# A two-pass projection for the eight decay and gate columns of a hybrid decoder layer

## The chip, the cores and the metric

The kernel runs on one core of a Trainium2 chip. The core has a matrix engine (PE, with its weight loads shown apart as PEld), three engines for work on vectors (DVE, ACT and POOL) and sixteen DMA engines. In this kernel nearly all DMAs are issued from the queue of a fifth engine, SP. The engines run side by side and wait for one another through semaphores. The metric is the device time of one execution in microseconds (us); lower is better.

## The reference

One decoder layer with a sequence of 2048 tokens and 1024 channels. One input projection feeds two kinds of mixers, four heads each: a gated delta rule (GDN) and HGRN2. After them come the output projection, an MLP of width 4096 and a gated embedding. The columns that this case is about are `a_gdn` and `b_gdn`, four each: they become the decay and the gate of the four GDN heads.

```python
hn = rms_norm(h, pre_mix_norm[i])
proj = jnp.einsum('btd,dc->btc', hn, w_in[i]).astype(f32)
qkv = proj[..., OFF_GDN_QKV:OFF_GDN_Z]
a_gdn = proj[..., OFF_GDN_A:OFF_GDN_B]          # 4 columns
b_gdn = proj[..., OFF_GDN_B:OFF_HG_F]           # 4 columns
...
beta = jax.nn.sigmoid(b_gdn)
g_dec = -jnp.exp(gdn_a_log[i]) * jax.nn.softplus(a_gdn + gdn_dt_bias[i])
o_a = gated_delta_rule_chunked(q_a, k_a, v_a, g_dec, beta)
...
o_b = hgrn2_chunked(jax.nn.silu(q_hg), k_b, i_hg, log_f)
```

Everything is float32.

## The kernel before

**Products in parts.** A float32 operand is split into a high part `t[:, 0]`, rounded to the PE's format, and a low part `t[:, 1]`, the rest (`split`, line 164 on ACT and line 165 on DVE). A product of 128 output columns, 1024 input channels and 512 tokens takes for each of the eight blocks `k` of 128 channels three matmuls of 128x512: high weight with high input, high weight with low input, low weight with high input. That is 24 matmuls into one PSUM bank.

**Quarters and works.** The tokens are cut into four quarters of 512. The loop over `works` (lines 1053 to 1077) makes, for each quarter, 33 such products: first `ab`, the eight columns for decays and gates (padded to 128: the decays in rows 0 to 3 of the result, the gates in rows 32 to 35), and then, for each head number `h` from 0 to 3, the eight products k, q, v, z of a GDN head and f, i, q, g of an HGRN2 head. The result of a work lies in one of two PSUM banks (`pm`, two buffers), so the work after the next can start only when the bank has been read.

**Ticks.** Every work has `SPT = 3` steps of eight matmuls, and after each step `tick()` (with `half()` in the middle of it) runs what the agenda holds for this moment: a mixer is a generator, each of its pieces issues instructions, and lists of offsets (`A_STEPS` for the GDN mixer, `B_STEPS` for the HGRN2 mixer) say at which tick after the head's first work each piece stands. Thus the small matmuls of the mixers are placed by hand among the large ones. A mixer runs on for up to 64 ticks, that is 40 ticks into the 24 of the next head; the mixers of head 3 run into the next quarter, through its `ab` work and the works of its head 0.

**Order on the engines.** The order of PE's instructions, and that of SP's DMAs within the loop, is as written. On ACT, DVE and POOL a planner puts the instructions in order by its own estimate of when each can run. Once it is fixed, each engine takes its instructions in that order.

**What stands around the start of a quarter.** `decays` (lines 493 to 524) takes the `ab` result: two ACT reads of the PSUM bank (`sp`, line 498, and the gates' tanh, line 500), then a short chain that changes between DVE and ACT (`se`, lines 502 to 504, with two loads of function tables on ACT; `sp`, lines 505 and 506), a running sum on DVE (line 508), a store `gd`, a reordered copy `gbb` (line 515) and four transposes on PE (line 519). At the same ticks the last mixers of the quarter before are still in the middle. GDN head 3 does its triangular solve on DVE (`pr_g` and `xs_g`, lines 698 to 703), stores it (`xd_g`, line 708), loads it back in another layout (`xt_g`, line 715), transposes it on DVE (`xn_g`, line 717) and multiplies on PE (`psp_g`, line 722). GDN head 2 finishes (`og_g` line 585, `osq_g` line 587, `hl_g` line 165, then the matmuls `nrm_g`, lines 270 and 271). The new quarter's first convolution reads its bank with three DVE instructions (`acc_kg`, line 542).

**Weights.** In quarter 0 each work's weights are loaded raw, split, and written to DRAM as a high and a low part of 512 KB each (`cache_...<-w`); the later quarters load these 1024 KB back (`reload`). Three buffers `whl` hold weights; the weights of work `j + 2` are asked for at the start of work `j`.

Of the kernel before, what the change touches and what calls it, by code (L numbers as in the profile page):

```python
# [10 lines left out]
F32 = mybir.dt.float32  # L11
F32R = mybir.dt.float32r
BF16 = mybir.dt.bfloat16
U32 = mybir.dt.uint32
AF = mybir.ActivationFunctionType
ALU = mybir.AluOpType
# [4 lines left out]
P = 128  # L21
T = 2048
D = 1024
KD = D // P
QT = 512
# [63 lines left out]
def trunk(ctx, tc, x, xT, pT, vecs, w_in, w_ab, gdn_a_log, gdn_dt_bias, w_out, w_up, w_down,  # L89
# [345 lines left out]
    with mixers as mctx:  # L435
# [45 lines left out]
        def stage(name, src, k=KD):  # L481
# [8 lines left out]

            return ready

        def decays(ps, q):

            gb = mt(f"gb_{q}", "gb", 1, (36, QT))
            sp = m2.tile([4, QT], F32, tag="tmp", name=f"sp_{q}")
            se = m2.tile([4, QT], F32, tag="th", name=f"se_{q}")
            S.activation(sp, ps[0:4, :], AF.Identity, bias=dec[:, 1:2])
            V.memset(gb, 0.0)
            S.activation(gb[32:36, :], ps[32:36, :], AF.Tanh, scale=0.5)  # L500
            V.tensor_scalar(gb[32:36, :], gb[32:36, :], 0.5, 0.5, ALU.mult, ALU.add)
            V.scalar_tensor_tensor(se, sp, -1.0, sp, ALU.mult, ALU.max)
            S.activation(se, se, AF.Exp, scale=-1.0)
            S.activation(se, se, AF.Ln, bias=1.0)
            V.scalar_tensor_tensor(sp, sp, 0.0, se, ALU.max, ALU.add)
            V.tensor_scalar(sp, sp, nexpa, None, ALU.mult)
            for c in range(NC):
                V.tensor_tensor_scan(gb[0:4, blk(c)], one[0:4, :], sp[:, blk(c)], 0.0, ALU.mult, ALU.add)
            gd = dr.tile([4, QT], F32, name=f"gd{q}")
            decay[q] = [gd, None]  # L510
            yield
            nc.sync.dma_start(gd, gb[0:4, :])
            yield
            back = mt(f"gbb_{q}", "gbb", 1, (36, QT // 2))
            V.tensor_copy(back.rearrange("p (n b i) -> p n b i", b=NB, i=SB), odd_back(gb))
            yield
            ps = bank(f"ps_gb_{q}", ph)
            for c in range(NC):
                PE.transpose(ps[:, c * 36 : (c + 1) * 36], back[:, blk(c // 2)] if c % 2 else gb[:, blk(c)],
                             ident[:36, :36])  # L520
            gcol = sm.tile([P, NC, 36], F32, tag="gcol", name=f"gcol_{q}", bufs=2)
            V.tensor_copy(gcol.rearrange("p c n -> p (c n)"), ps[:, : NC * 36])
            V.tensor_scalar(gcol[:, :, 4:8], gcol[:, :, 0:4], -1.0, None, ALU.mult)
            decay[q][1] = gcol
# [426 lines left out]
        for q in range(NQ):  # L951
            works.append((f"ab{q}", "ab", w_ab, q, None, None, None, None))
            for h in range(4):
                g, b = {}, {}
                t = SPT * len(works)
                for j, then in KINDS:
                    works.append((f"{j}_{q}_{h}", f"in{j + h}", w_in[j + h], q, h, then, g, b))
                a_steps, b_steps = (A_LAST, B_LAST) if (q, h) == (NQ - 1, 3) else (A_STEPS, B_STEPS)
                if h:
                    a_steps = A_AHEAD + a_steps[2:]  # L960
                elif q == 0:
                    a_steps = A_FIRST + a_steps[len(A_FIRST) :]
                at(t, gdn_mixer(q, h, g), a_steps)
                at(t, turn_i(q, h, b), I_STEPS)
                at(t, hgrn_mixer(q, h, b), b_steps)
# [3 lines left out]
        def stage_work(j):  # L969

            if j < len(works) and works[j][3] == 0:
                staged[j] = stage(works[j][0], works[j][2])

        def split_work(j):

            if j < len(works):
                split_w[j] = staged.pop(j)() if j in staged else reload(works[j][1], works[j][0])

        def keep_work(j):
            if works[j][3] == 0:  # L980
                keep(works[j][1], split_w[j])

        def load_x(q):

# [53 lines left out]
                for k, n in enumerate(names):  # L1038
                    sumd[n, g] = c, k

        per_q = SPT * (1 + 8 * 4)
        starts = [per_q * q + 5 + n * i for q, m, n in ((1, 6, 14), (2, 5, 16), (3, 5, 16)) for i in range(m)]
        for g, t in enumerate(starts):
            at(t, down_sums(g), (0, 4, 6, 10))
# [7 lines left out]
        with tc.manual_schedule(engines={mybir.EngineType.SP}):  # L1052
# [5 lines left out]
            for j, (name, key, src, q, h, then, g, b) in enumerate(works):  # L1058
# [4 lines left out]
                w, xt = split_w.pop(j), xts[q]  # L1063
                terms = []
                for k, xk in enumerate(xt):
                    terms += [(w[:, 0, k, :], xk[:, 0, :]), (w[:, 0, k, :], xk[:, 1, :]), (w[:, 1, k, :], xk[:, 0, :])]
                nt = len(terms)
                for s in range(SPT):
                    for i in range(s * nt // SPT, (s + 1) * nt // SPT):
                        if i == (2 * s + 1) * nt // (2 * SPT):  # L1070
                            half()
                        PE.matmul(ps, *terms[i], start=i == 0, stop=i == nt - 1)  # L1072
                    if s == SPT - 1 and h is None:
                        at(clock[0], decays(ps, q), (0, 2, 3, 5) if q else (0, 2, 4, 7))
                    tick()
                    if s == SPT - 1 and h is not None:
                        then(ps, q, h, g, b)

            qs = (2, 3)
# [752 lines left out]
```

## Time and profile before

The three runs gave 2724.35, 2725.19 and 2733.05 us; the median is 2725.19 us. The profiled execution has a span of 2719.9 us from the first instruction to the last. No time beside its span is given for that execution; the median lies 5.3 us above the span.

| engine | busy us | share of the span | instructions |
|---|---|---|---|
| PE | 2660.8 | 98% | 12745 |
| PEld | 2215.1 | 81% | 12745 |
| DVE | 2040.8 | 75% | 4219 |
| ACT | 1464.0 | 54% | 2940 |
| POOL | 118.5 | 4% | 133 |

The works of the projection run from 40 us to 1064 us. The `ab` works begin at 40.2, 285.5, 544.05 and 805.4 us. The rest of the span is output projection, MLP and gate.

How to read it: a row of the timeline has the start in us, the duration in us, the engine, the line, the operation, what it writes and reads, its shape, and in brackets how long the engine sat idle before it and what ended that. A row of waits has who waited for whom, the total in us, how often, and the longest. A row of windows has the stretch, its length, and then for each engine the busy time in it. A PE row with "x16" is a run of sixteen matmuls.

### The profile page before, as it was taken

How to read it: one execution, taken by the hardware profiler on the slowest of the kernel's cores; microseconds unless marked ns; L12 is line 12 of the kernel's file. 1: busy time of each engine (PE TensorE's matmuls, PEld its weight loads, DVE VectorE, ACT ScalarE, POOL GpSimd, SP SyncE). 2: the span in 40 equal slices, each digit the busy share in tenths (PEclk: the TensorE clock that was granted, in tenths of full speed). 3: DMA queues.
4: the chain of work that ended last, by engine and by line, in shares of the span. 5: the costliest groups of instructions: out<-in, count | busy, mean ns of one | idle time of the engine just before them, and what ended most of it. 6: DMA issues, size and time to landing. Idle time of an engine off the chain costs nothing.

```text
span 2719.9 us, 38475 instructions
## 1 busy us (share of the span) xinstructions
PE 2660.8 (98%) x12745; PEld 2215.1 (81%) x12745; DVE 2040.8 (75%) x4219; ACT 1464.0 (54%) x2940; POOL 118.5 (4%) x133
## 2 busy tenths in 40 slices
PE   8999999999999999998999999999999999999999
PEld 6788888888888887876788888888888888888887
DVE  7778878787777777576989867768787765567776
ACT  7665555465445455575655646555555545465432
POOL 0000000000000000011000000001000000001000
PEclk9999999999999999998999999999999999999999
DMA  8777777667666665887566457667454346577663
GB/s 282 273 237 255 236 263 242 216 214 241 213 201 221 223 213 164 271 281 231 177 232 228 175 178 240 216 202 244 164 196 163 139 172 207 193 256 247 216 212 131
DMA packets 268742, 589.24 MB, mean 217 GB/s; under 512 B 55658, under 2 KB 60232, under 8 KB 249344
## 3 DMA queue, kind: packets, MB, share of 16 engines
q1 hardware_dynamic: 266240, 582.59, 63.9%
q0 software_dynamic: 2304, 4.20, 0.9%
q8 instruction: 101, 1.65, 0.3%
q14 instruction: 97, 0.79, 0.1%
HBM read 419.75 MB, written 166.92 MB: 216 GB/s over the span
## 4 chain that ended last, share of the span: by engine, by line
PE 51%; DMA 3%; DVE 3%; issue 3%; ACT 1%; POOL 1%; SPq 0%; POOLq 0%; DVEq 0%; ACTq 0%
PE d L1143 22%; PE u L1143 22%; PE mmg L1143 6%; PE mmo L1143 1%; DMA raw_out<-in_w_out_dram 1%; DMA yo<-in_xT_dram 0%; PE mme L191 0%; POOL acc_y L234 0%; DMA b<-h1d 0%; DMA w_out<-cache_out 0%; DMA db<-hid 0%; DVE t L165 0%; DMA h1d<-yo 0%; POOL yo L1229 0%; DVE pr_g L698 0%
## 5 line engine op out<-in xcount | busy, mean ns | idle before, releaser
L1072 PE MATMUL mm<-xt,w 128*128 128x512 f32 x3072 | 784.1, 400 | 1.4 <-ACT zt_zg L577 1.1
L1072 PEld LDWEIGHTS mm<-xt,w 128*128 128x128 f32 x3072 | 553.3, 189 | 102.3 <-ACT zt_zg L577 1.5
L1143 PE MATMUL d<-db,da 128*128 128x512 f32 x2688 | 611.0, 389 | 0.5 <-ACT db L217 0.2
L1143 PE MATMUL u<-t,wu 128*128 128x512 f32 x2604 | 591.1, 389 | 0.0
L1143 PEld LDWEIGHTS d<-db,da 128*128 128x128 f32 x2688 | 504.3, 188 | 106.4 <-DVE db L218 1.0
L1143 PEld LDWEIGHTS u<-t,wu 128*128 128x128 f32 x2604 | 488.7, 188 | 101.5
L218 DVE TENSOR_TENSOR db<-db 128x512 fp32r<-128x512 f32 x224 | 159.9, 714 | 72.4 <-ACT db L217 71.7
L1495 DVE TENSOR_TENSOR u<-u,u 128x512 f32<-128x512 f32 x224 | 150.2, 681 | 58.1 <-PE u L1143 56.6
L1143 PE MATMUL mmo<-mixT,w_out 128*128 128x512 f32 x720 | 173.4, 402 | 11.8 <-DMA w_out<-cache_out 5.5
L217 ACT ACTIVATE db<-db 128x512 fp32r<-128x512 f32 x224 | 140.9, 629 | 78.2 <-DMA db<-hid 71.9
L1143 PEld LDWEIGHTS mmo<-mixT,w_out 128*128 128x128 f32 x720 | 139.5, 195 | 44.6 <-DMA w_out<-cache_out 5.9
L1143 PE MATMUL mmg<-h2T,wg 128*128 128x512 f32 (+1 forms) x792 | 174.8, 383 | 0.0
L1538 ACT ACTIVATE u<-u 128x512 f32<-128x512 f32 x128 | 80.8, 631 | 166.3 <-DVE u L1495 166.0
L1143 PEld LDWEIGHTS mmg<-h2T,wg 128*128 128x128 f32 x792 | 145.5, 188 | 29.1
L165 DVE TENSOR_TENSOR da<-da 128x512 fp32r<-128x512 f32 x128 | 93.7, 732 | 77.7 <-ACT da L164 77.1
L164 ACT ACTIVATE da<-da 128x512 fp32r<-128x512 f32 x128 | 80.5, 629 | 124.8 <-DMA da<-sumd 91.6
L164 ACT ACTIVATE wu<-a 128x512 fp32r<-128x512 f32 x124 | 75.0, 623 | 44.3 <-DMA a<-in_w_up_dram 43.0
L698 DVE TENSOR_TENSOR pr_g<-xs_g,sys_g 128x16 f32<-128x16 f32 (+14 forms) x240 | 94.4, 393 | 5.6
L165 DVE TENSOR_TENSOR wu<-a,wu 128x512 fp32r<-128x512 f32 x124 | 85.6, 693 | 10.8 <-ACT wu L164 10.5
L234 POOL TENSOR_TENSOR acc_y<-acc_y,sq_y 128x512 f32<-128x512 f32 x28 | 38.5, 1374 | 1261.6 <-ACT sq_y L233 1260.8
L1539 ACT ACTIVATE u<-u 128x512 f32<-128x512 f32 x128 | 80.5, 629 | 3.1
L165 DVE TENSOR_TENSOR da<-dr,da 128x512 fp32r<-128x512 f32 x96 | 66.3, 691 | 19.0 <-ACT da L164 16.5
(385 smaller groups left out, 3792.6 us busy)
## 6 DMA issues: line engine op xcount, KB each, us to landing
w<-cache_in SPq DMA_DIRECT2D x96, 1024.0 KB
db<-hid SPq DMA_DIRECT2D x224, 256.0 KB
cache_in<-w SPq DMA_DIRECT2D x32, 1024.0 KB
hid<-u SPq DMA_DIRECT2D x128, 256.0 KB
da<-sumd SPq DMA_DIRECT2D x128, 256.0 KB
a<-in_w_up_dram SPq DMA_DIRECT2D x124, 256.0 KB
hid<-ht SPq DMA_DIRECT2D x96, 256.0 KB
dr<-in_w_down_dram SPq DMA_DIRECT2D x96, 256.0 KB
```

Source lines behind the costliest of these rows:

```text
L164: S.activation(t[:, 0], raw, AF.Copy)
L165: eng.tensor_tensor(t[:, 1], raw, t[:, 0], ALU.subtract)
L217: S.activation(t[:, 0], plain(t), AF.Copy)
L218: V.tensor_tensor(t[:, 1], plain(t), t[:, 0], ALU.subtract)
L234: eng.tensor_tensor(acc, acc, sq, ALU.add)
L698: V.tensor_tensor(pr[:, :, :, 0:i], xs[:, None, :, 0:i].broadcast_to([P, 2, GC, i]), sys[:, 0:i, i : i + 2].rearrange("p j two -> p two j" ...
L1072: PE.matmul(ps, *terms[i], start=i == 0, stop=i == nt - 1)
L1143: PE.matmul(ps, a, b, start=start, stop=stop)
L1495: V.tensor_tensor(c[new], c[old], ps, ALU.add)
L1538: S.activation(c[k], c[k], AF.Relu)
L1539: S.activation(c[k], c[k], AF.Square)
```

## The change

The `ab` work's weight tile now holds the high parts of 64 columns in its columns 0 to 63 and the low parts of the same 64 columns in columns 64 to 127. One matmul thus multiplies both by an input; two matmuls per block (high input, low input) make the work, 16 in place of 24. Rows 0 to 35 of the result hold the products of the high weights, rows 64 to 99 those of the low weights, and `decays` adds them: ACT copies the second part to SBUF (`ab_rest`), DVE adds it to the first (`ab`), and the ACT instructions that read PSUM before now read this sum. The tile is stored once and loaded back with 512 KB in place of 1024 KB, and the raw load takes 64 of the 128 columns.

The `ab` work has two ticks in place of three. The start of each head is moved with it (`t`), and so is the length of a quarter (`per_q`). What is counted from the start of a quarter and is no part of a head (the norms of the embedding in quarter 0, the loads `x_scale`, the sums `down_sums`) keeps its offset from there, and so stands one tick later against the heads.

```diff
+        def stage_ab():
+            raw = wp.tile([P, KD, P // 2], F32, tag="raw", name="raw_ab0", bufs=2)
+            nc.sync.dma_start(raw, w_ab[:, :, : P // 2])
+            def ready():
+                w = wp.tile([P, KD, P], F32R, tag="whl", name="w_ab0")
+                S.activation(w[:, :, : P // 2], raw, AF.Copy)
+                V.tensor_tensor(w[:, :, P // 2 :], raw, w[:, :, : P // 2], ALU.subtract)
+                return w
+            return ready
+
+        def keep_ab(w):
+            cached["ab"] = dr.tile([P, KD * P], F32, name="cache_ab")
+            nc.sync.dma_start(cached["ab"], w.bitcast(F32).rearrange("p k n -> p (k n)"))
+
+        def reload_ab(q):
+            w = wp.tile([P, KD, P], F32R, tag="whl", name=f"w_ab{q}")
+            nc.sync.dma_start(w.bitcast(F32).rearrange("p k n -> p (k n)"), cached["ab"])
+            return w
+
         def decays(ps, q):
             gb = mt(f"gb_{q}", "gb", 1, (36, QT))
-            sp = m2.tile([4, QT], F32, tag="tmp", name=f"sp_{q}")
+            rest = m2.tile([36, QT], F32, tag="th", name=f"ab_rest_{q}")
+            ab = m2.tile([36, QT], F32, tag="tmp", name=f"ab_{q}")
             se = m2.tile([4, QT], F32, tag="th", name=f"se_{q}")
-            S.activation(sp, ps[0:4, :], AF.Identity, bias=dec[:, 1:2])
+            S.activation(rest, ps[P // 2 : P // 2 + 36, :], AF.Copy)
+            V.tensor_tensor(ab, ps[:36, :], rest, ALU.add)
+            sp = ab[0:4, :]
+            S.activation(sp, sp, AF.Identity, bias=dec[:, 1:2])
             V.memset(gb, 0.0)
-            S.activation(gb[32:36, :], ps[32:36, :], AF.Tanh, scale=0.5)
+            S.activation(gb[32:36, :], ab[32:36, :], AF.Tanh, scale=0.5)
...
-                t = SPT * len(works)
+                t = SPT * len(works) - (q + 1)
...
-                staged[j] = stage(works[j][0], works[j][2])
+                staged[j] = stage_ab() if works[j][4] is None else stage(works[j][0], works[j][2])
...
-                split_w[j] = staged.pop(j)() if j in staged else reload(works[j][1], works[j][0])
+                if j in staged:
+                    split_w[j] = staged.pop(j)()
+                elif works[j][4] is None:
+                    split_w[j] = reload_ab(works[j][3])
+                else:
+                    split_w[j] = reload(works[j][1], works[j][0])
...
-                keep(works[j][1], split_w[j])
+                if works[j][4] is None:
+                    keep_ab(split_w[j])
+                else:
+                    keep(works[j][1], split_w[j])
...
-        per_q = SPT * (1 + 8 * 4)
+        per_q = SPT * (1 + 8 * 4) - 1
...
                 for k, xk in enumerate(xt):
+                    if h is None:
+                        terms += [(w[:, k, :], xk[:, 0, :]), (w[:, k, :], xk[:, 1, :])]
+                        continue
                     terms += [(w[:, 0, k, :], xk[:, 0, :]), (w[:, 0, k, :], xk[:, 1, :]), (w[:, 1, k, :], xk[:, 0, :])]
                 nt = len(terms)
-                for s in range(SPT):
-                    for i in range(s * nt // SPT, (s + 1) * nt // SPT):
-                        if i == (2 * s + 1) * nt // (2 * SPT):
+                steps = nt // KD
+                for s in range(steps):
+                    for i in range(s * KD, (s + 1) * KD):
+                        if i == s * KD + KD // 2:
                             half()
                         PE.matmul(ps, *terms[i], start=i == 0, stop=i == nt - 1)
-                    if s == SPT - 1 and h is None:
+                    if s == steps - 1 and h is None:
                         at(clock[0], decays(ps, q), (0, 2, 3, 5) if q else (0, 2, 4, 7))
                     tick()
-                    if s == SPT - 1 and h is not None:
+                    if s == steps - 1 and h is not None:
                         then(ps, q, h, g, b)
```

## The prediction

> **What bounds the kernel now.** I read the page first, then the busy time in stretches, then PE's waits by stretch, then the timeline of each engine around the start of a quarter.
>
> ```profile
> span 2719.9 us, 38475 instructions
> PE 2660.8 (98%) x12745; PEld 2215.1 (81%) x12745; DVE 2040.8 (75%) x4219; ACT 1464.0 (54%) x2940; POOL 118.5 (4%) x133
> ```
> ```profile
> core 0: us, PE busy (x) PEld busy (x) DVE busy (x) ACT busy (x) POOL busy (x), PEclk, DMA share, GB/s
> ...
> 544.00:585.00 41.00, 38.95 (x210) 32.32 (x210) 34.78 (x95) 26.19 (x65) 3.25 (x4) 1.00 0.57 183
> 585.00:805.00 220.00, 216.01 (x1188) 183.73 (x1187) 164.57 (x490) 111.22 (x298) 11.34 (x13) 1.00 0.70 230
> 805.00:845.00 40.00, 38.64 (x209) 32.04 (x208) 33.81 (x93) 26.29 (x65) 3.67 (x4) 1.00 0.52 182
> ```
>
> PE is the bound over the whole span. But the start of a quarter is a place of its own: in the 41 us from 544 DVE is busy for 34.78 us (85%), against 164.57 of 220 (75%) in the stretch behind it, and PE is idle for 5% of it against 2%. The clock granted is 1.00 throughout. PE's waits there name DVE and ACT. In order: one in the start of quarter 0, two in that of quarter 1, two in that of quarter 2, one in that of quarter 3:
>
> ```profile
> PE mm L1072 <- DVE acc_kg L542: 0.3, 1, 0.3
> ```
> ```profile
> PE psp_g L722 <- DVE xn_g L717: 1.4, 1, 1.4
> PE kk_g L659 <- ACT y_qg L551: 0.2, 1, 0.2
> ```
> ```profile
> PE kk_g L659 <- ACT y_qg L551: 1.0, 1, 1.0
> ...
> PE psp_g L722 <- DVE xn_g L717: 0.4, 1, 0.4
> ```
> ```profile
> PE kk_g L659 <- ACT y_qg L551: 0.4, 1, 0.4
> ```
>
> The reader is to see that PE already waits where head 3 of the quarter before needs `xn_g` from DVE. That is the place into which the change pushes the new quarter's work.
>
> **Part 1: 32 matmuls less.** Eight in each of four quarters, with no other PE work added.
>
> ```profile
> 77.88 18.42 PE L1072 MATMUL mm<-xt,w 128*128 128x512 f32 x80
> ```
> ```profile
> 569.38 3.90 PE L1072 MATMUL mm<-xt,w 128*128 128x512 f32 x16
> ```
> ```profile
> L1072 PE MATMUL mm_ab<-xt,w_ab x96: 388/389/500, 40.2 to 812.0; 128*128 128x512 f32 x96
> ```
>
> A run's length is the steps between starts plus one duration of 0.39: (18.42 - 0.39)/79 = 0.228 us a step, (3.90 - 0.39)/15 = 0.234. With 0.231 a quarter saves 1.85 us and all four 7.4 us, where PE is the only bound. The Trainium skill (TensorE: Matmul & The Clock Gate, Back-to-back issue gap) gives about 131 ns for a sustained N=512 matmul; by that figure the saving would be an estimated 4.2 us. The two rows here contradict it.
>
> **Part 2: a longer chain behind `ab`.** Added per quarter: one ACT copy and one DVE add of 36x512, and ACT's `sp` and tanh now wait for DVE. I walk through quarter 2 with the order of the changed program's DVE and the durations of these rows:
>
> ```profile
> 550.98 0.43 ACT L826 ACTIVATE hb_h<-qk_h 128x256 f32<-128x256 f32 x1 [3.60 <-DVE qk_h L824]
> 551.31 0.67 ACT L498 ACTIVATE sp<-mm_ab,dec 4x512 f32<-4x512 f32 x1
> 552.00 0.59 ACT L500 ACTIVATE gb<-mm_ab 4x512 f32<-4x512 f32 x1
> 552.61 1.28 ACT L503 ACT_TABLE_LOAD   x1
> 555.24 0.63 ACT L503 ACTIVATE se<-se 4x512 f32<-4x512 f32 x1 [1.35 <-DVE se L502]
> 555.90 0.37 ACT L771 ACTIVATE w_g<-psb_g,cc_g 128x128 f32<-128x128 f32 x1
> 556.28 1.28 ACT L504 ACT_TABLE_LOAD   x1
> 557.58 0.63 ACT L504 ACTIVATE se<-se 4x512 f32<-4x512 f32 x1
> ```
> ```profile
> 551.85 0.59 DVE L698 TENSOR_TENSOR pr_g<-xs_g,sys_g 128x224 f32<-128x224 f32 x1
> ...
> 554.54 0.67 DVE L502 SCALAR_TENSOR_TENSOR se<-sp 4x512 f32<-4x512 f32 x1
> ...
> 558.24 0.68 DVE L505 SCALAR_TENSOR_TENSOR sp<-sp,se 4x512 f32<-4x512 f32 x1 [1.32 <-ACT se L504]
> ...
> 561.51 0.42 DVE L717 STREAM_TRANSPOSE xn_g<-xt_g 128x256 f32<-128x256 f32 x1
> 561.87 0.68 DVE L860 COPY_PREDICATED att_h<-cst,at_h 128x256 f32<-128x256 uint32 x1
> 562.37 0.29 DVE L776 SCALAR_TENSOR_TENSOR S_g<-S_g,cd_g,psc_g 128x128 f32<-128x128 f32 x1
> 562.60 0.66 DVE L585 TENSOR_TENSOR og_g<-pso_g,zt_zg 128x512 f32<-128x512 f32 x1
> 563.20 0.66 DVE L587 TENSOR_TENSOR osq_g<-osq_g,q_g 128x512 f32<-128x512 f32 x1
> 563.79 0.27 DVE L515 COPY gbb<-gb 36x256 f32<-36x256 f32 x1
> 563.99 0.73 DVE L542 SCALAR_TENSOR_TENSOR acc_kg<-mm,cols,acc_kg 128x509 f32<-128x509 f32 x1
> 564.65 0.67 DVE L165 TENSOR_TENSOR hl_g<-osq_g,hl_g 128x512 fp32r<-128x512 f32 x1
> ```
> ```profile
> 561.99 0.71 PE L722 MATMUL psp_g<-xn_g,um 128*128 128x128 f32 x4 [0.38 <-DVE xn_g L717]
> ```
>
> The changed order on DVE, from the chain's `sp` to `xn_g` (its lines are moved by 27):
>
> ```
> L532 ab  L869 att_h  L533 ab  L871 att_h  L535 gb x4  L882 qk_h  L887 att_h  L542 gbb
> L569 acc_kg  L280 m_h  L803 S_g  L569 acc_kg  L612 og_g  L744 xn_g
> ```
>
> ACT still takes `hb_h` first, so the copy runs from 551.31 for some 0.6 us (row of line 500). DVE takes the add behind `pr_g`, at 552.35; a 512-wide add lasts 0.60 to the next start (562.60 to 563.20). ACT's `sp` starts at 553.0, not 551.31; the tanh and the table load (0.59 and 1.28) end at 555.6, and `se` at 555.24 moves to 555.6. ACT loses only the 1.35 us for which it sat idle. The chain ends 0.35 us late and DVE starts `sp` at 558.6: the 1.85 us by which `ab` ends earlier is gone here. Queued behind the waiting ACT instructions are `w_g` and the table load alone, so nothing else pays.
>
> **Part 3: all offsets moved.** Head 3's pieces keep their distance in matmuls from the quarter's start; the new quarter's works come 1.85 us earlier among them. Before, `xn_g` stood 3.27 us behind the chain's `sp` (558.24 to 561.51). Now the predicated copy (0.50 to the next start), `gbb` (0.20), two of `acc_kg` (0.66 each), `S_g` (0.23) and `og_g` (0.60) stand ahead of it: 2.85 us more. So `xn_g` starts at 558.6 + 3.27 + 2.85 = 564.7 and `psp_g` 0.48 later, at 565.2 against 561.99. PE pays 3.2 us and has saved 1.85: 1.35 us lost. Late next is `nrm_g`, which needs the two parts of `hl_g`; the changed order of ACT puts a table load (1.28) and `y_kg` ahead of its high part, so this costs between 0 and 1.3 us. The later wait of 1.0 us for `y_qg` should vanish, since PE comes later and ACT does not. I take +0.6 us for quarter 2 (1.35 less 1.0, and a little of `nrm_g`), between -1.85 (no new wait) and +2.65 (nothing won back).
>
> Quarters 1 and 3 have the same new order. In quarter 1 `xn_g` was already late by 1.4, 1.0 more than in quarter 2, so about 1.0 less is added: 0.35 lost, 0.2 to win back, and a little of `nrm_g`: I take +0.5, between -1.85 and +1.65. In quarter 3 the wait was 0.4, as in quarter 2, and only 0.4 for `y_qg` can be won back: 1.35 - 0.4 = +1.0, between -1.85 and +2.65. In quarter 0 there is no older head. There PE waits 0.3 for the bank that `acc_kg` reads: DVE sets the pace there too, so the 1.85 us cannot stand in full. The add (0.60) and the split of one more weight tile now come ahead of the last read of that bank. Between -1.85 (nothing waits) and +1.85 (the bank comes as much later as `ab` ends earlier) I take +0.3, the wait that exists.
>
> **Part 4: moved data.** The cached tile is 512 KB smaller in one store and three loads, issued from the same places on SP; the DMA share is 0.57 at quarter 2's start, so I cost this at 0 (the cover is two works of lead; without it a load of half the size could only come sooner). The raw load has pieces of 256 bytes; ACT's split of it comes without a wait today, 0 again. That split is half as wide on ACT and DVE: 0 to -0.5 us before the first `ab`; I take -0.1 with the rest of the sum. What is not tied to heads comes a tick later: 0, between -1 and +1.
>
> Sum: 0.3 + 0.5 + 0.6 + 1.0 = 2.4, with part 4 some 2.3 us. The profiled span 2719.9 would become 2722.2. The median of the runs lies 5.3 above the span: 2727.5 us against 2725.19. Within 0.3% (8.2 us), about what a measurement of this kernel can tell, this is no change.
>
> **The rivals.**
> *The saving stands.* PE stays the only bound, -7.4 us: 2717.8. If the new order also ends the waits shown at the starts (0.3 + 1.4 + 0.2 + 1.0 + 0.4 and another 0.4 for `xn_g` in quarter 3: 3.7), it is 2714.1. For it: PE's 98%, and waits at the starts of 0.3 to 1.4 us. Against it: the order on DVE. It decides if `xn_g` still comes within 0.5 us of when PE wants it.
> *Slower: the load of `xt_g`.* In the changed order of SP a weight load of 1024 KB is asked for between the store `xd_g` and the load `xt_g`, in each of the three later starts; before, it came behind both.
>
> ```profile
> 554.65 0.32 SPq L708 DMA_DIRECT2D xd_g<-xs_g  x1
> ...
> 556.24 1.75 SPq L715 DMA_DIRECT2D xt_g<-xd_g  x4
> ```
>
> The add puts the last `xs_g` and so `xd_g` some 1.6 us later. Store to load took 1.6 us with quiet queues, the four issues 1.75. If the 1024 KB go ahead (at 183 to 230 GB/s, 4.6 to 5.7 us), `xt_g` lands at 563 to 567, against 564.7 when DVE wants it. DVE would then stand still, with all behind `xn_g`. At 3 us late in three quarters: 9 + 2.3, that is 2736.5. It decides from 2 us late on.
> *Same waits, all won back later in the heads:* 2721 to 2725, within the forecast's range.
>
> **How the numbers follow.** The forecast, with won-back waits in it, has 0.40 and a range of its own from 2720 to 2734 (the upper bounds of the four quarters sum to 8.8 us); 0.03 of it lies beyond 8.2 us. The saving stands: 0.27, of which 0.17 beyond 8.2 us, since 7.4 alone lies within. The late load: 0.33, beyond 8.2 us. So faster 0.17, slower 0.33 + 0.03 = 0.36, no change 0.37 + 0.10 = 0.47. The range, 2714.5 to 2740, takes in most of both rivals.
>
> **What would show it.** PE has 32 matmuls less. At the starts of quarters 1 to 3 `psp_g` waits for `xn_g` 3 us or more (right), under 0.5 (the saving stands), or `xn_g` itself waits for DMA `xt_g` (the late load). `se` of line 504 ends within 0.5 us of where it did, counted from the `ab` work's first matmul. In quarter 0 PE waits for `acc_kg` 1 us or more. The prediction is wrong if the second half of a quarter, where I move nothing, changes by over 2 us: the planner's new order reaches far into the heads.

## The result and the profile after

The changed kernel took 2736.33 us (median of 15 runs, 2729.60 to 2742.37); the kernel before, run beside it, took 2726.78 (15 runs, 2718.84 to 2733.91). The ratio is 1.0036, with a 95% interval of 1.0025 to 1.0046: slower by 9.6 us.

The page of the changed kernel, span and engines:

```profile
span 2727.4 us, 38417 instructions
PE 2656.4 (97%) x12713; PEld 2213.1 (81%) x12713; DVE 2038.8 (75%) x4223; ACT 1466.0 (54%) x2944; POOL 119.2 (4%) x133
```

The 32 matmuls are gone (12745 to 12713) and the span is longer. The run that was profiled took 2729.6 us, 2.2 more than its span and the lowest of the 15; so the spans, 7.5 us apart, understate the loss a little.

The busy time in stretches: the start of quarter 2 and the start of quarter 3 (columns as before: PE, PEld, DVE, ACT, POOL, the clock granted to PE, the DMA share, GB/s):

```profile
549.60:590.60 41.00, 36.66 (x195) 30.84 (x194) 34.85 (x94) 26.67 (x66) 3.30 (x4) 0.96 0.55 177
...
809.60:849.60 40.00, 35.68 (x173) 29.58 (x172) 32.54 (x90) 25.32 (x62) 2.99 (x3) 0.91 0.59 182
```

PE is busy for 36.66 of the first 41 us where it was busy for 38.95, DVE does as much as before, and the clock granted is no longer 1.00. PE's waits there, of the changed kernel: two in the start of quarter 0, then the one of quarter 1, and the largest of quarter 2 (quarter 3 shows the same 3.9):

```profile
PE mm L1111 <- DVE m_e L280: 3.3, 1, 3.3
PE mm L1111 <- DVE acc_vg L569: 1.9, 1, 1.9
...
PE psp_g L749 <- DVE xn_g L744: 3.3, 1, 3.3
...
PE psp_g L749 <- DVE xn_g L744: 3.9, 1, 3.9
```

To see where the time went I measure each quarter's start by two marks that every kernel has: the first matmul of `ab`, and the first `psx_g` of the quarter's own head 0, some 80 to 99 us later. Here are the two marks of quarters 0 and 3 on PE's timeline, before and then after:

```profile
40.22 5.73 PE L1072 MATMUL mm_ab<-xt,w_ab 128*128 128x512 f32 x24 [0.21 <-ACT sq_e L233]
121.94 0.61 PE L722 MATMUL psx_g<-part,xt_g 128*128 128x128 f32 x4
...
805.41 0.40 PE L1072 MATMUL mm_ab<-xt,w_ab 128*128 128x512 f32 x1
...
897.80 0.61 PE L722 MATMUL psx_g<-part,xt_g 128*128 128x128 f32 x4
```
```profile
39.33 3.93 PE L1111 MATMUL mm_ab<-xt,w_ab 128*128 128x512 f32 x16 [0.21 <-ACT sq_e L233]
...
125.41 0.61 PE L749 MATMUL psx_g<-part,xt_g 128*128 128x128 f32 x4
...
809.63 0.40 PE L1111 MATMUL mm_ab<-xt,w_ab 128*128 128x512 f32 x1
...
905.30 0.61 PE L749 MATMUL psx_g<-part,xt_g 128*128 128x128 f32 x4
```

The start of quarter 0 took 121.94 - 40.22 = 81.72 us and now takes 86.08; that of quarter 3 took 92.39 and now takes 95.67. All four, in us:

| | quarter 0 | quarter 1 | quarter 2 | quarter 3 | sum |
|---|---|---|---|---|---|
| before | 81.72 | 93.56 | 93.04 | 92.39 | 360.7 |
| after | 86.08 | 95.00 | 94.18 | 95.67 | 370.9 |
| more | +4.36 | +1.44 | +1.14 | +3.28 | +10.2 |

In these two executions the whole loss lies in the starts. Elsewhere 0.9 us are gained ahead of the first `ab` and 2.1 between the starts and the end of the projection, and 0.3 lost behind it: 10.2 - 0.9 - 2.1 + 0.3 = 7.5, the difference of the spans.

How the 10.2 us come about can be read from PE's busy time between the same marks. Here are its sums over the four starts, in windows from mark to mark: before, after, and for comparison e11, an experiment told below that leaves out the 32 matmuls and adds nothing:

```profile
sum 360.71, PE 351.44 PEld 293.34 DVE 285.04 ACT 209.69 POOL 20.74; mean PE 87.86 PEld 73.33 DVE 71.26 ACT 52.42 POOL 5.19
```
```profile
sum 370.93, PE 352.45 PEld 295.62 DVE 285.54 ACT 210.12 POOL 20.19; mean PE 88.11 PEld 73.90 DVE 71.39 ACT 52.53 POOL 5.05
```
```profile
sum 359.43, PE 344.30 PEld 287.09 DVE 284.00 ACT 208.97 POOL 20.82; mean PE 86.08 PEld 71.77 DVE 71.00 ACT 52.24 POOL 5.20
```

PE sits idle for 9.3 us before and for 18.5 us after, 9.2 more. Its busy time ought to fall by the 32 matmuls. In e11, whose starts run at the full clock, it falls by 7.1 us. In the changed kernel it grows by 1.0: the work that is left took 8.2 us longer than in e11. Seven windows of 3.41 us in these starts have the clock at 0.50, two each in quarters 0, 1 and 3 and one in quarter 2. In quarter 0 single rows show it: behind its two long waits, eight matmuls of 128x512 take 3.32 and 3.63 us, where before they took 2.09 and 2.11. So the loss has two parts of like size, more waiting and a slower PE behind the waits.

### The profile page after: what moved, and what is told of

It reads as the page before. It is cut to its first block, busy times and chain, and to the rows that moved or that the text cites. A ratio compares the mean times of both kernels' runs of the same rounds, so it can differ in the third digit from the quotient of the medians.

```text
span 2727.4 us, 38417 instructions
## 1 busy us (share of the span) xinstructions
PE 2656.4 (97%) x12713; PEld 2213.1 (81%) x12713; DVE 2038.8 (75%) x4223; ACT 1466.0 (54%) x2944; POOL 119.2 (4%) x133
## 4 chain that ended last, share of the span: by engine, by line
PE 55%; DVE 5%; DMA 5%; issue 3%; ACT 1%; POOL 1%; SPq 0%; POOLq 0%; DVEq 0%; ACTq 0%
PE u L1182 22%; PE d L1182 21%; PE mmg L1182 6%; PE mm L1111 4%; DMA raw_out<-in_w_out_dram 1%; PE mmo L1182 1%; DMA sys_g<-ud_g 1%; DMA rd_g<-m_g 1%; DVE pr_g L725 1%; POOL acc_y L234 1%; DVE xs_g L728 0%; DMA ud_g<-u_g 0%; DMA yo<-in_xT_dram 0%; DVE xs_g L730 0%; PE at_h L880 0%
```

## The experiments

Each ratio is against the kernel before, run on the same chip in the same hour; that kernel's own median was between 2715.3 and 2726.8 us from one set to the next, so times of different sets are not compared. The last columns are the lengths of the four starts as above, from one profiled execution each.

| kernel | offsets | ratio (95% interval) | q0 | q1 | q2 | q3 |
|---|---|---|---|---|---|---|
| e11: 16 matmuls | before's | 0.9999 (0.9990 to 1.0007) | 80.97 | 92.57 | 93.05 | 92.84 |
| e1: 16 matmuls, copy, add | before's | 1.0036 (1.0022 to 1.0050) | 82.71 | 94.46 | 96.30 | 96.42 |
| e2: 24 matmuls | moved | 1.0021 (1.0012 to 1.0031) | 89.36 | 94.03 | 92.32 | 91.58 |
| e3: 16 matmuls | moved | 1.0017 (1.0006 to 1.0028) | 85.39 | 91.42 | 94.50 | 95.03 |
| the change: 16, copy, add | moved | 1.0036 (1.0025 to 1.0046) | 86.08 | 95.00 | 94.18 | 95.67 |
| e12: 16, copy, add with the bias | moved | 1.0037 (1.0024 to 1.0050) | 85.17 | 93.27 | 95.96 | 95.42 |
| e4: before, xn_g late | before's | 1.0028 (1.0019 to 1.0038) | 82.14 | 94.50 | 95.08 | 97.86 |
| e5: the change, psp_g later | moved | 1.0048 (1.0033 to 1.0063) | 83.88 | 95.36 | 98.68 | 95.60 |
| e6: e5, quarter 0 in three ticks | q0 before's | 1.0040 (1.0027 to 1.0053) | 81.82 | 95.36 | 95.60 | 97.55 |
| e7: e1, psp_g later | before's | 1.0025 (1.0014 to 1.0036) | 82.49 | 96.63 | 95.42 | 94.42 |
| e8: before, psp_g later | before's | 1.0035 (1.0022 to 1.0048) | 82.42 | 95.50 | 94.20 | 93.94 |
| e9: the change, waits filled | moved | 1.0050 (1.0035 to 1.0065) | 85.35 | 98.54 | 93.11 | 92.86 |
| e10: before, waits behind it filled | before's | 1.0001 (0.9992 to 1.0010) | 81.88 | 94.64 | 94.10 | 92.68 |

How far a start can be trusted: e10 has the order of before up to 1060 us, and its starts differ from before's by 0.16, 1.08, 1.06 and 0.29 us. So a difference of under about 1 us in one start says nothing. The sum of the four differs by 2.6 us between these two executions, that of the parts between the starts by 4.8.

### The parts of the change, one by one

e1 keeps the new arithmetic and undoes the moved ticks:

```diff
-                t = SPT * len(works) - (q + 1)
+                t = SPT * len(works)
...
-        per_q = SPT * (1 + 8 * 4) - 1
+        per_q = SPT * (1 + 8 * 4)
...
-                steps = nt // KD
+                steps = SPT        # 16 matmuls as 5, 5 and 6
...
```

> The two-pass arithmetic alone (16 matmuls, the copy and the add), with the ab work cut into three ticks of 5, 5 and 6 matmuls and all offsets as before the change. Theory 'moved ticks': the loss comes from the new quarter's DVE work standing one tick earlier against the old heads; then this kernel has waits of psp_g for xn_g under 2 us at the starts of quarters 1 to 3, a granted clock of 1.00 through the projection, and 2717 to 2724 us. Theory 'chain': the loss comes from the copy and the add ahead of the decays; then psp_g still waits 3 us or more, the clock falls to 0.5 behind it as in the changed kernel, and the time is 2732 to 2740 us.

e2 is the reverse, the moved ticks with the arithmetic of before:

```diff
-                t = SPT * len(works)
+                t = SPT * len(works) - (q + 1)
...
-        per_q = SPT * (1 + 8 * 4)
+        per_q = SPT * (1 + 8 * 4) - 1
...
-                for s in range(SPT):
+                steps = 2 if h is None else SPT        # 24 matmuls as 12 and 12
+                for s in range(steps):
...
```

> The moved ticks alone: the arithmetic of before (24 matmuls, no copy, no add), but the ab work in two ticks of 12 matmuls and all offsets as in the changed kernel. Theory 'moved ticks': xn_g stands behind 2 to 3 us more of DVE work, and PE comes to psp_g 1.85 us later than before; psp_g waits 1.5 us or more at the starts of quarters 1 to 3, and the time is 2729 us or more. Theory 'chain': without the add the decays' chain ends as early as before, psp_g waits under 1 us, the clock stays at 1.00 through the projection, and the time is within 3 us of before.

e3 leaves the copy and the add out of the changed kernel, and e11 out of e1, so that the products with the low weights do not reach the result:

```diff
-            S.activation(rest, ps[P // 2 : P // 2 + 36, :], AF.Copy)
-            V.tensor_tensor(ab, ps[:36, :], rest, ALU.add)
-            sp = ab[0:4, :]
-            S.activation(sp, sp, AF.Identity, bias=dec[:, 1:2])
+            S.activation(sp, ps[0:4, :], AF.Identity, bias=dec[:, 1:2])
...
-            S.activation(gb[32:36, :], ab[32:36, :], AF.Tanh, scale=0.5)
+            S.activation(gb[32:36, :], ps[32:36, :], AF.Tanh, scale=0.5)
```

> The changed kernel without the copy and the add: the decays and gates are read from the PSUM rows of the high weights, as before, and the products with the low weights are left out of the result. 16 matmuls and two ticks stay. Theory 'chain': psp_g waits under 1.5 us, no fall of the granted clock in the projection, 2716 to 2722 us. Theory 'moved ticks': the wait stays at 3 us or more with the clock at 0.5 behind it in at least two of the three later starts, 2731 us or more.

> The 32 matmuls less alone: the ab work has 16 matmuls in three ticks (5, 5 and 6), all offsets are those of before, and there is no copy and no add (the products with the low weights are computed and left out of the result). Against the run with the two-pass arithmetic in three ticks it differs by the copy and the add alone. Theory 'saving stands': PE is the bound also at the starts, and 7.4 us go: 2714 to 2717 where before has 2722, a ratio of 0.9973 to 0.9985. Theory 'slack': at the starts the works of DVE and ACT set the time, and the matmuls taken away come back as waits of psa_g, psp_g and the banks: within 0.1% of before, or slower.

**What was measured.** e1: 2732.13 against 2721.23 us, 1.0036; psp_g waits 1.7, 2.5 and 2.5 us, and the clock halves at two of the three starts. It fits neither theory in full: the time is the chain's, the waits are between. e2: 2728.09, 1.0021; the time is 0.9 us short of what the theory of the moved ticks had, and the place is another. Its waits for xn_g at the three later starts are 1.6, 0.8 and 1.0, and it loses 7.6 us in the start of quarter 0, where two windows are at half clock:

```profile
PE mm L1073 <- ACT zt_zg L577: 2.8, 1, 2.8
PE psp_g L722 <- DVE xn_g L717: 2.2, 1, 2.2
PE mm L1073 <- DVE w L165: 2.1, 2, 1.6
```

e3: 2727.14, 1.0017, with waits of 1.0, 3.3 and 3.3 for xn_g: even without the copy and the add, and with 32 matmuls less, it is slower than before, by less than the one theory and more than the other had. e11: 2714.02 against 2715.29 us on its chip, 0.9999, as the theory of slack had it.

**What follows.** e11 has 32 matmuls less, a smaller weight tile, nothing added, and no gain; a gain of 7.4 us, or of 4.2, lies outside its interval (-2.7 to +1.9 us). The start of quarter 2 shows why. PE's waits there, of e11:

```profile
PE psa_g L787 <- DVE S_g L799: 1.9, 1, 1.9
PE psp_g L745 <- DVE xn_g L740: 1.3, 1, 1.3
PE kk_g L682 <- ACT y_qg L574: 0.4, 1, 0.4
```

That is 3.6 us; before had 1.0 (`y_qg`), 0.4 (xn_g) and 0.5 (S_g), so 1.9. Of the 1.85 us saved 1.7 come back as waits. Over all four starts PE's idle time grows from 9.3 to 15.1 us, so that 5.9 of the 7.1 us come back. But e11 is not the old order with a gap in it. The planner has dealt out DVE's work anew: `og_g`, `osq_g`, the small `S_g` and one more predicated copy, which before stand behind xn_g, stand ahead of it:

```profile
559.28 0.67 DVE L608 TENSOR_TENSOR og_g<-pso_g,zt_zg 128x512 f32<-128x512 f32 x1
...
560.48 0.42 DVE L740 STREAM_TRANSPOSE xn_g<-xt_g 128x256 f32<-128x256 f32 x1
```

xn_g starts 18.25 us behind the first `ab` matmul, 0.80 later than before, though the chain's `se` ends 0.9 earlier. So in the order that e11 got, DVE and ACT set the length of a start; whether 7.4 us could be had with before's order no run shows. With the copy and the add, e1 has in the same place:

```profile
PE psp_g L749 <- DVE xn_g L744: 2.5, 1, 2.5
PE psa_g L791 <- DVE S_g L803: 1.9, 1, 1.9
PE kk_g L686 <- ACT y_qg L578: 1.0, 1, 1.0
```

That is 1.8 us more. In quarters 2 and 3 e1 has the same pieces ahead of xn_g as e11 and the add besides, and xn_g comes 1.3 to 1.5 us later: 0.7 to 0.9 us more of DVE work and 0.6 of standing idle. Over e11, the copy and the add cost 0.37% with the old offsets (e1) and, on top of e3, 0.19% with the moved ones. The moved ticks cost 0.21% with the old arithmetic, 0.18% with 16 matmuls, and nothing on top of e1. The parts do not add up; each of them makes the planner deal out a new order on DVE and ACT.

**Quarter 0** is where the moved ticks cost most. All kernels with two ticks in quarter 0 need 83.9 to 89.4 us for its start, all with three ticks 81.0 to 82.7. The timelines of DVE, ACT and PE of the changed kernel show how:

```profile
55.92 0.73 DVE L569 SCALAR_TENSOR_TENSOR acc_kg<-mm,cols,acc_kg 128x510 f32<-128x510 f32 x1
56.97 1.23 DVE L165 TENSOR_TENSOR w<-raw,w 128x1024 fp32r<-128x1024 f32 x1 [0.32 <-ACT w L164]
58.11 0.74 DVE L569 SCALAR_TENSOR_TENSOR acc_kg<-mm,cols,acc_kg 128x511 f32<-128x511 f32 x1
```
```profile
55.88 1.06 ACT L164 ACTIVATE w<-raw 128x1024 fp32r<-128x1024 f32 x1 [1.36 <-DMA cache_in<-w]
```
```profile
59.00 3.32 PE L1111 MATMUL mm<-xt,w 128*128 128x512 f32 x8 [3.29 <-DVE m_e L280]
```

A later work's weight split now stands between the second and the third of DVE's reads of the `acc_kg` bank; before, it stood ahead of the first. DVE's half of it waits for ACT's half, and that for the store of an older weight tile. PE waits 3.29 us for the bank (the page names `m_e`, the small instruction behind the read).

### Is it the length of the decays' chain?

e12 puts the bias into the add, so that ACT's `sp` and two handovers fall away (`dec` is widened to 36 rows, zero from row 4 on).

```diff
...
-            V.tensor_tensor(ab, ps[:36, :], rest, ALU.add)
-            sp = ab[0:4, :]
-            S.activation(sp, sp, AF.Identity, bias=dec[:, 1:2])
+            V.scalar_tensor_tensor(ab, ps[:36, :], dec[:, 1:2], rest, ALU.add, ALU.add)
+            sp = ab[0:4, :]
```

> The changed kernel with the bias of the decays put into the add on DVE (one instruction adds the two PSUM parts and the bias for all 36 rows), so that ACT's sp of 36 or 4 rows and its two handovers between DVE and ACT fall away: 0.72 us of ACT and some 1.0 us of waiting less in the chain, the add itself stays. The result is that of the reference. Theory 'chain': the copy and the add cost 5 us (the changed kernel against the run without them) because the chain of the decays ends later; most of it comes back, ratio 1.0017 to 1.0025. Theory 'order': what costs is the place of xn_g and of the old heads' pieces in the order of DVE, which this leaves as it is; the ratio stays at 1.003 to 1.004.

1.0037: nothing comes back. Its waits for xn_g are 1.6, 3.2 and 3.2. This does not settle the question of the heading, for the order did not stay as it was. DVE in quarter 2, from the chain's end to xn_g:

```profile
560.76 0.68 DVE L532 SCALAR_TENSOR_TENSOR ab<-ab,se 4x512 f32<-4x512 f32 x1 [1.52 <-ACT se L531]
...
567.13 0.73 DVE L569 SCALAR_TENSOR_TENSOR acc_kg<-mm,cols,acc_kg 128x511 f32<-128x511 f32 x1
567.79 0.67 DVE L614 TENSOR_TENSOR osq_g<-osq_g,q_g 128x512 f32<-128x512 f32 x1
568.39 0.42 DVE L744 STREAM_TRANSPOSE xn_g<-xt_g 128x256 f32<-128x256 f32 x1
```

The chain did get shorter: `se` ends 13.59 us behind the first `ab` matmul, 1.07 earlier than in the changed kernel. But the planner now takes the third `acc_kg` and `osq_g`, 1.3 us of work, ahead of xn_g, which starts 0.3 us later than there. What was won in the chain was filled with other pieces. What a shorter chain would bring with the order kept isn't known.

### A wait of known size

e4 makes xn_g late in the kernel before, by copies that change nothing:

```diff
+            for _ in range((1, 3, 6, 0)[q] if h == 3 else 0):
+                V.tensor_copy(flat(xn), flat(xt))
             V.transpose(flat(xn), flat(xt))
```

> The kernel before, with 1, 3 and 6 copies of xt_g into xn_g (128x256, some 0.3 us each, other DVE work between them) ahead of the transpose of head 3 of quarters 0, 1 and 2, so that xn_g comes later by three doses at the starts of quarters 1, 2 and 3. Nothing else changes. Theory 'clock': where the wait of psp_g stays under 2 us the granted clock stays at 1.00 and the start loses what the wait grows; where it passes some 3 us (quarter 3, 6 copies) the clock is 0.5 for 3.4 us or more behind it and the start loses 1.7 us or more beyond the wait. Theory 'wait only': the clock does not follow the wait, and each start loses its wait alone. In all 2728 to 2734 us.

The waits became 2.1, 2.4 and 4.7 us (from 1.4, 0.4 and 0.4: 7.0 more), the time 2727.8 against 2721.23, 6.6 more and just under the range expected. The clock halved behind all three, behind the wait of 2.1 too. There is no sharp threshold near 2 us: in quarter 1 a wait of 1.7 (e1) and one of 1.6 (e12) left it at 1.00, and one of 1.6 (e2) did not. The starts grew by 0.9, 2.0 and 5.5 us, 8.5 in all and 1.4 more than this wait. Within them PE's idle time grew by 4.8 us, since other waits became shorter, and PE's work took 0.9, 1.1 and 1.7 us longer, with four windows of 3.41 us at half clock. Neither theory fits whole: each window slowed PE by some 0.9 us, but little beyond the wait was lost, because a later PE waits less for others.

### Moving psp_g out of its wait

e5 takes the changed kernel, e7 takes e1, e8 the kernel before, and each gets the same lines; e6 is e5 with three ticks for the `ab` work of quarter 0 alone.

```diff
...
+                if h == 3 and q < 3:
+                    a_steps = a_steps[:16] + (24, 25, 27, 31, 33, 34, 36) + a_steps[23:]
                 at(t, gdn_mixer(q, h, g), a_steps)
```
```diff
-                t = SPT * len(works) - (q + 1)
+                t = SPT * len(works) - q
...
-                steps = nt // KD
+                steps = 2 if h is None and q else SPT
...
```

> The changed kernel; head 3 of quarters 0 to 2 loads xt_g and transposes it one tick earlier and does psp_g one tick (8 matmuls, 1.85 us) later. No work is added or left out. Theory 'clock': PE still waits for psp_g at the starts of quarters 1 to 3, but some 0.5 to 1.5 us in place of 3.3 to 3.9; no 3.41 us window has PE idle for over half of it, the granted clock stays at 1.00 at these starts, and each start gains the wait (2.5 us) and 1.7 to 3.4 us of slow matmuls: 10 to 16 us less than the changed kernel, so about 2 to 7 us less than before on this chip. Theory 'wait only': 2 to 2.5 us a start, 6 to 8 us less than the changed kernel, so about before's time.

> As the run with psp_g later, but the ab work of quarter 0 alone has three ticks (5, 5 and 6 matmuls) and the offsets of quarter 0 are those of before; quarters 1 to 3 keep two ticks. Theory 'moved ticks cost quarter 0': the waits of 3.3 and 1.9 us for the banks of acc_kg and acc_vg and the two half-clock windows behind them go, and quarter 0 is 2 to 3 us shorter than in the changed kernel: 2 to 3 us less than the run with psp_g later. Theory 'copy and add cost quarter 0': quarter 0 stays as long as in the changed kernel, and the two runs are within 1 us.

> The run with the two-pass arithmetic alone (three ticks of 5, 5 and 6 matmuls, offsets of before), with head 3 of quarters 0 to 2 loading xt_g one tick earlier and doing psp_g one tick later. Theory 'clock': the waits of 1.7 to 2.5 us for xn_g fall under 1 us, the two half-clock windows at the starts go, and the time falls by 6 to 10 us from that run's 2732; the waits of psa_g for S_g (1.4 to 1.9 us) stay, so it ends at 2722 to 2726. Theory 'wait only': 4 to 6 us less.

> The kernel before with the same move of head 3's pieces and nothing else: it tells how much of the gain of the others is the move's own. Its waits for xn_g are 1.4, 0.4 and 0.4 us with the clock at 1.00, so by both theories no more than 2.1 us can go: 2719 to 2722 where before has 2721.

Measured: e5 1.0048, e6 1.0040, e7 1.0025, e8 1.0035. The waits of psp_g for xn_g did go in e5 and e6, and the next instructions wait instead. PE's waits in the start of quarter 2, of e5:

```profile
PE psd_g L749 <- ACT part L777: 2.8, 1, 2.8
PE nrm_g L270 <- ACT hl_g L164: 2.0, 1, 2.0
PE at_h L880 <- ACT keys_h L885: 1.0, 1, 1.0
```

Both theories fall for e5: 5.8 us are waited in these three where the changed kernel waited 4.5 in all. The wait for xn_g is only the first place at which PE meets the lateness of DVE and ACT. e8 says the same of the kernel before: moving four pieces of one head, with no work added, costs 0.35%, where neither theory allowed a loss. In quarter 1 its second psp_g, which needs a small copy into xn_g, waits 3.1 us where before's did not wait; but its profiled execution (span 2723.4) doesn't show the whole of the loss, so where the rest goes is open. e6 against e5 shows 2.1 us less in the start of quarter 0, as expected of the moved ticks; the ratios differ by as much, within their intervals. e7 fell by 0.11% (3.0 us) against e1, less than either theory had.

### Keeping PE busy in its waits

e9 puts 12 matmuls that nothing uses ahead of psp_g in the changed kernel; e10 does so in the kernel before at five waits behind the projection.

```diff
...
+            for i in range(12 if h == 3 and q < 3 else 0):
+                xk = xts[q + 1][i % KD]
+                PE.matmul(b5, xk[:, 0, :P], xk[:, 0, :], start=True, stop=True)   # psp_g overwrites b5
```
```diff
...
             ps = bank(f"mmo_{q}_{d}", pp)
+            for _ in range({8: 7, 23: 12, 24: 20}.get(j, 0)):
+                PE.matmul(ps, xin[q][0][:, 0, :P], xin[q][0][:, 0, :], start=True, stop=True)
...
```

> The changed kernel with 12 idle-time matmuls (128x512, 0.231 us each, 2.8 us in all) put ahead of psp_g of head 3 in quarters 0 to 2, where PE waits 3.3 to 3.9 us for xn_g. They write the bank that psp_g then overwrites; their result is used by nothing. The wait does not get shorter: PE only has something to do in it. Theory 'clock': no 3.41 us window has PE idle for over half of it there, the five half-clock windows behind the three later starts go (5 x 1.7 us in the profiled execution of the changed kernel), the mean granted clock rises from 0.992 to 0.995, and the time falls by 6 to 9 us from the changed kernel's 1.0036 of before: a ratio of 1.0003 to 1.0014. Theory 'lateness only': the clock follows something else or costs nothing because DVE is the bound, and the ratio stays at 1.003 to 1.004.

> The kernel before with the same kind of matmuls, used by nothing, at five places behind the projection where its PE waits 1.8 to 5.5 us: 6 and 11 ahead of two of the last head's at_h products, 7, 12 and 20 ahead of the output projection's works 8, 23 and 24. The waits are not shortened. Theory 'clock': the half-clock windows between 1077 and 1272 us (seven, 23.9 us long in the profiled execution of before) go for the most part, the mean clock rises from 0.996 to 0.998 or more, and the time falls by 4 to 9 us: a ratio of 0.9967 to 0.9985. Theory 'lateness only': within 0.1% of before.

The clock did what was expected: at the filled waits it stays at 1.00 in e9, and in e10's profiled execution it is 1.000 over the whole span. The times did not: 1.0050 and 1.0001. Of e9's starts, those of quarters 2 and 3 are shorter than in the changed kernel, by 1.1 and 2.8 us, and within 0.5 us of before's. That is what the half clock was read to cost there: PE's work had taken 0.8 and 2.3 us longer. But the filling also made the planner change the order behind psp_g (head 2's `og_h` now ahead of two small copies into xn_g), and quarter 1 lost 3.5 us: its second psp_g waits for those copies:

```profile
PE psp_g L749 <- DVE xn_g L773: 3.4, 1, 3.4
```

Quarter 0's start was not filled and keeps its loss (3.6 us over before). In e10 the profiled execution takes 4.8 us less from the projection's last matmul to the first of the MLP (244.8 against 249.6), yet it is 7.1 us longer up to there, in the order of before, and the median of 11 runs is before's; what takes the gain back isn't settled. No version that beats both kernels came out of this: e11 is level with before and leaves out the low weights.

## Why the prediction was right or wrong

The range (2714.5 to 2740) holds 2736.33, and "slower" had 0.36 against 0.47 for "no change". The forecast, +2.3 us, was too small by 7.3. That the range holds is luck: the walk's own range ended at 2734, its upper bounds at +8.8 us, and only the rival of the late load, whose cause isn't there, carried it to 2740.

**Part 1, the 7.4 us.** The sum charged this saving with waits that ate it, and so it is: in e11 PE has 7.1 us less to do in the starts, waits 5.9 more, and the time stays. The rival "the saving stands" falls for the orders that the planner dealt out. The estimate of 4.2 us by the figure of the Trainium skill (TensorE: Matmul & The Clock Gate, Back-to-back issue gap) falls with it, though not by its figure: whatever a matmul costs, nothing was saved where the other engines came late. Ending the reading at PE's 98% would have missed that; the 85% of DVE at a start was the better sign.

**Part 2, the chain.** Right in quarters 2 and 3: the second `se` ends 14.66 us behind the first `ab` matmul, 0.50 later than before (0.35 forecast). Wrong in quarter 1, where it ends 2.3 us later: DVE takes the add 1.45 us after ACT's copy is done. The copy and the add as a whole cost 5 to 10 us over kernels without them (e3 and e11), which the forecast has nowhere as a term. In e1 against e11 the starts grow by 10.5 us, 6.8 of them waits and 3.6 PE work that takes longer. e12 cannot tell how much of it is the chain, since its order changed too. That a new order alone can cost as much is shown by e2 and e8, which add no work; that it is what the copy and the add cost is argued, not shown.

**Part 3, psp_g.** The walk held. DVE, then ACT, PE and SP of the changed kernel in quarter 2:

```profile
557.96 0.68 DVE L523 TENSOR_TENSOR ab<-mm_ab,ab_rest 36x512 f32<-36x512 f32 x1
...
564.36 0.68 DVE L532 SCALAR_TENSOR_TENSOR ab<-ab,se 4x512 f32<-4x512 f32 x1 [2.62 <-ACT se L531]
...
570.01 0.67 DVE L612 TENSOR_TENSOR og_g<-pso_g,zt_zg 128x512 f32<-128x512 f32 x1
570.61 0.42 DVE L744 STREAM_TRANSPOSE xn_g<-xt_g 128x256 f32<-128x256 f32 x1
```
```profile
563.70 0.63 ACT L531 ACTIVATE se<-se 4x512 f32<-4x512 f32 x1
```
```profile
571.09 0.88 PE L749 MATMUL psp_g<-xn_g,um 128*128 128x128 f32 x4 [3.91 <-DVE xn_g L744]
```
```profile
562.05 0.37 SPq L185 DMA_DIRECT2D w<-cache_in  x1
...
563.21 1.75 SPq L742 DMA_DIRECT2D xt_g<-xd_g  x4
```

Here psp_g starts 571.09 - 549.67 = 21.42 us behind the first `ab` matmul; forecast were 565.2 - 544.05 = 21.15. The wait of 3 us or more that was to show it is there in all three quarters (3.3, 3.9, 3.9), and the waits for `y_qg` are gone. The sign named for the late load isn't there: the weight load does stand between `xd_g` and `xt_g`, but DVE takes xn_g straight behind `og_g`, without a wait for a DMA. That rival's 2736.5 was the time that came, for another reason.

**What failed.** First, the clock. The sum counted waits against matmuls saved and put the clock at nothing; its reading had "the clock granted is 1.00 throughout". The changed kernel's own waits halve it. Against before, in us:

| | quarter 0 | quarter 1 | quarter 2 | quarter 3 | sum |
|---|---|---|---|---|---|
| PE's idle time grows, less the 1.85 saved | +1.30 | -0.83 | +0.34 | +1.01 | +1.8 |
| forecast | +0.3 | +0.5 | +0.6 | +1.0 | +2.4 |
| PE's busy time grows, with the 1.85 added back | +3.05 | +2.28 | +0.80 | +2.27 | +8.4 |
| forecast | 0 | 0 | 0 | 0 | 0 |

What the walk did count came out near it in sum, if not in each quarter; the whole miss is the last term, 1.2 us for each of the seven windows of 3.41 us at half clock, at most 1.7 if PE is busy throughout. The split is one of accounts, for a slower PE also waits less for others. e9 tests it in two starts: with the clock kept at 1.00 those of quarters 2 and 3 fall to before's length. In all e9 gained no time, as quarters 0 and 1 lost what they did.

Second, **quarter 0**, mis-sized by far: +0.3 forecast, with +1.85 as the upper bound, and +4.36 measured. For the bank of `acc_kg` the bound was right: the matmul that waits for it starts 19.67 us behind the first `ab` matmul, 17.87 before, 1.80 more, and the sign named for it is there (a wait of 3.29). The weight split ahead of the last read was in the prediction too. What it missed comes behind: the clock halves there and again behind the wait for `acc_vg`, and twice eight matmuls take 2.75 us longer. The other waits about make up for one another. e6 shows that all this goes with the ticks: with three in quarter 0 that start is 81.82 us, without a half-clock window.

Third, **Part 4**, "what is not tied to heads: 0, -1 to +1", has no run of its own; e2, which loses 7.6 us in the start of quarter 0, moves the heads as well. In the parts behind the starts the change gained 2.1 us where 0 was forecast. The sign named for it (over 2 us) is met by quarter 2's second part, 2.5 us shorter, but e10, in before's order, differs by 1.4 to 1.8 in three such parts, so this shows little.

Last, 5.3 us were added to the span for what lies beside it. The runs show 1.8 to 2.2; the rest was that the profiled execution of before lies below the median of its runs.

## What to carry to other kernels

An engine that is 98% busy over a span need not be the bound in the stretch that an edit touches: take the work away there alone, with nothing added, and see whether the time moves, before paying for the saving with work on another engine. A new wait of PE can have two prices, the wait and the slower clock behind it; here they were of like size, and PE's busy time between two marks tells the second. Where a planner deals out the order, a move of a few offsets can cost as much as the edit itself (0.2 to 0.35% here), so each edit needs its placement tried again. Its parts are judged by kernels that differ in one part, and only after looking whether the order stayed the same: in e11 and e12 it did not.

## What the runs showed of the hardware that was not expected

**The clock falls on short waits.** The changed kernel, in windows of 3.41 us on the raster on which its clock changes, around psp_g in quarter 1, and the window of before that holds its wait of 1.4 us:

```profile
305.25:308.67 3.42, 0.16 (x1) 0.00 (x0) 3.42 (x11) 0.42 (x1) 1.17 (x1) 1.00 0.32 46
308.67:312.08 3.41, 3.37 (x14) 2.98 (x15) 3.41 (x9) 2.06 (x5) 0.00 (x0) 0.50 0.79 298
312.08:315.49 3.41, 3.41 (x9) 2.64 (x9) 1.71 (x6) 2.02 (x6) 0.00 (x0) 0.50 0.78 195
315.49:318.90 3.41, 3.41 (x22) 3.02 (x22) 2.23 (x5) 3.38 (x10) 0.00 (x0) 1.00 0.75 231
```
```profile
302.91:306.32 3.41, 2.41 (x15) 2.17 (x16) 3.37 (x9) 1.56 (x4) 0.00 (x0) 1.00 0.86 319
```

The clock granted is 1.00 or 0.50 for whole windows. In e4 a wait of 2.1 us sufficed:

```profile
303.08:306.49 3.41, 1.31 (x10) 1.13 (x10) 3.05 (x9) 1.06 (x3) 0.00 (x0) 1.00 0.88 306
306.49:309.90 3.41, 3.41 (x10) 2.66 (x9) 3.41 (x8) 1.80 (x6) 0.00 (x0) 0.50 1.04 295
```

I laid this raster over all fourteen profiled executions, from 30 to 2600 us. Of the windows at full clock in which PE was idle for 1.92 us or more, all 64 were followed by one at 0.50; of those with 1.54 to 1.91 us, 13 of 45; of those with 0.9 to 1.53, 3 of 145. So the clock follows whether PE was idle for somewhat over half of a window, and a wait of 2 to 3 us costs it or not by where it falls on the raster: two waits of 2.2 us in e5's quarter 0 left it at 1.00. The Trainium skill (TensorE: Matmul & The Clock Gate, What's actually happening) has the free-running window of 3413 ns, and the traces agree, with changes on a raster of 3.41 us. The same section of the Trainium skill gives an idle window of some 3.4 us as the condition for the half clock; here 1.92 us in a window were enough.

**What a window at half clock costs.** I set PE's busy time in each start of the thirteen other executions against before's, with 0.231 us for each matmul fewer or more. In 25 starts without such a window it differs by -0.7 to +1.0 us, in 17 with one by +0.7 to +2.0, in 10 with two by +1.7 to +3.2. Behind the projection the price isn't settled: e10 raised the mean granted clock of its runs from 0.996 to 0.998, and the time stayed (1.0001).
